# A handicap in the order of issue for two kinds of TensorE work in the attention block of a two-block network

## The chip, the cores and the metric

The kernel runs on one core of one Trainium2 chip. The metric is the device time of one execution in microseconds (us). Three runs of the kernel before gave 1686.42, 1688.52 and 1691.94 us; their median is 1688.52 us.

The engines: PE is TensorE (matmuls and transposes), DVE is VectorE, ACT is ScalarE, POOL is GpSimd, SP issues the DMAs.

## The reference

A sequence of 256 tokens of width 1024 passes two layers of a first block and then two layers of a second one, all in float32. The change lies in the first block's mixer:

```python
h = rmsnorm(x, g_pre_mix[l])
z = jnp.einsum('bsd,de->bse', h, w_in[l])
z_moba, z_fox, z_fg, z_cq, z_ckv, z_kr, z_dil = jnp.split(z, SPLIT_POINTS, axis=-1)
qa, ka = apply_rope(qa, cos_h, sin_h), apply_rope(ka, cos_h, sin_h)
o_moba = moba_attention(qa, ka, va)
log_f = jax.nn.log_sigmoid(z_fg.astype(jnp.float32) + b_forget[l].astype(jnp.float32))
cum = jnp.cumsum(log_f, axis=1).transpose(0, 2, 1)
o_fox = blocked_causal_attention(qb, kb, vb, HEAD_DIM ** -0.5, cum)
...
o_mla = blocked_causal_attention(q_full, k_full, v_c, (MLA_NOPE_DIM + MLA_ROPE_DIM) ** -0.5)
qd, kd = apply_rope(qd, cos_h, sin_h), apply_rope(kd, cos_h, sin_h)
o_dil = dilated_mixture(qd, kd, vd)
mix = jnp.concatenate([from_heads(o_moba), from_heads(o_fox), from_heads(o_mla), from_heads(o_dil)], axis=-1)
x = x + rmsnorm(jnp.einsum('bse,ed->bsd', mix, w_out[l]), g_post_mix[l])
```

There are four attentions of four heads each: moba (with 256 tokens it is plain causal attention), fox (the one with forget gates; `cum` is added to its logits), mla, and dilated. Only moba's and the dilated one's queries and keys are rotated as whole 512-column tiles.

## The kernel before, in words

The tokens are two halves `h` of 128. Each float32 factor of a large matmul is split in a high and a low part, and a product is made of three matmuls in the faster float32 form (hidden state `hX`, weights `wh` and `wl`). ACT makes the high part of a unit of weights and DVE the low part, while PE multiplies; `raw` is the DMA's landing place. Transposes, scores, value products and the running sum are in plain float32.

In `block1` (L824) the projections come in this order, each for both halves: the columns of mla with the forget gates (356), moba's queries and keys, moba's and fox's values, fox's queries and keys, mla's up-projections, the dilated queries and keys, the dilated values. A chain of its own takes each result on. `qkchain` (L917) rotates a 512-column tile on DVE into a tile `z`, takes a PSUM bank, transposes `z` in four parts on PE and copies the bank to `T` on ACT. `cumchain` (L1011) makes the log of the forget gates (`lf`, 128x8), sums it along the tokens with three small matmuls against a triangle of ones in `cs`, and copies the sum to `cum` on ACT. `foxchain` (L1046) waits for `cum` (L1058), copies it beside the keys of its half, and transposes these.

`group` (L838) is the attention of some heads of one half: scores on PE, mask added and row maximum on DVE, exponentials on ACT, reciprocal and scaling on DVE, transposes on PE, copy on ACT; `attend` (L879) follows with value products on PE and the split of the result into `mH` and `mL`. moba and dilated have two groups per half, fox and mla one in the first half and two in the second. After the projections `w_out` (L1132) multiplies with the output weights: first moba's part of half 0, then fox's part of half 0, then both of half 1, then mla's and the dilated parts.

The order on the engines is not written out. `Order` (L116) runs all chains and picks one instruction after another by the smallest key, the estimated start plus a bias; each engine then executes its instructions in that order:

```python
def push(self, task, op):
    ready = self.deps(op)
    b = op.bias() if callable(op.bias) else op.bias
    self.n += 1
    heapq.heappush(self.heap, (self.start(op, ready) + b + task.bias, ready, self.n, op, task))
```

`start` (L153) is the later of the time at which the operands are ready and the time at which the engine is free. Projection matmuls have the bias `B_MAIN` = 0.02 (us); transposes and the running sum's matmuls have 0. L292 is the matmul, L296 the transpose, L309 any ACT operation; all of a kind share one line, so tiles tell them apart.

Of the kernel before, what the change touches and what calls it, by code (L numbers as in the profile page):

```python
# [18 lines left out]
P = 128  # L19
# [13 lines left out]
CST_CAU, CST_DIL, CST_U, CST_IC = 0, 128, 384, 640  # L33
# [243 lines left out]
def body(ctx, tc, x, positions, wu, wm, wq_up, wkv_up, rows, feat, gfeat, cst, cid, out, nsub=99):  # L277
    nc = tc.nc
# [7 lines left out]
    def view(t):  # L286
        return t if isinstance(t, bass.AP) else t[:]

    def mm(o, l, r, start, stop, bias=B_MAIN, fp32=False, half=None):
        o, l, r = view(o), view(l), view(r)  # L290
        c = (4 if fp32 else 1) * r.free_size() / 2400 + 0.0027
        return Op("e", c, (o,), (l, r), lambda: nc.tensor.matmul(o, l, r, start=start, stop=stop), bias, half)  # L292

    def tr(o, i):
        o, i = view(o), view(i)
        return Op("e", 0.1094, (o,), (i,), lambda: nc.tensor.transpose(o, i, idt[:, :P]))  # L296

    def act(o, i, f, bias_=0.0, **kw):
        o, i = view(o), view(i)
        c = (0.052 if i.tensor.name.startswith("bank") else 0.093) + i.free_size() / 1200  # L300
        ins, outs = [i], [o]
        for k in ("scale", "bias"):
            if k in kw and not isinstance(kw[k], float):
                c += 0.093
                ins.append(view(kw[k]))
        if "accum_out" in kw:
            c += 0.093
            outs.append(view(kw["accum_out"]))
        return Op("a", c, outs, ins, lambda: nc.scalar.activation(o, i, f, **kw), bias_, None, f)  # L309
# [23 lines left out]
    def stt(o, a, s, b, op0, op1):  # L333
        o, a, b = view(o), view(a), view(b)
        ap = not isinstance(s, float)
        return Op("d", 0.069 + o.free_size() / 960 + 0.061 * ap, (o,), (a, b) + ((view(s),) if ap else ()),
                  lambda: nc.vector.scalar_tensor_tensor(o, a, s, b, op0=op0, op1=op1))  # L337
# [44 lines left out]
    cs = one.tile([P, CST_N], F32, name="cs")  # L382
    idt = one.tile([P, 176], F32, name="idt")
# [151 lines left out]
    def hidden(n, h, i, src, g):  # L535

        hH, hL = halves(h)
        kb = []
        for j in range(2):
            kb.append((yield banks))  # L540
        for j in range(4):
            yield tr(kb[j % 2][:, j * P:(j + 1) * P], src[:, j * P:(j + 1) * P])

        def low(kt, o):
            yield stt(hL[:, kt, :], o, g[:, kt:kt + 1], hH[:, kt, :], OP.mult, OP.subtract)
            ck.set(ck.flag("h", n, h, kt))
            if kt % 4 >= 2:
                banks.put(kb[kt % 2])

        for j in range(4):  # L550
            kt, o = 4 * i + j, kb[j % 2][:, j * P:(j + 1) * P]
            yield act(hH[:, kt, :], o, AF.Copy, scale=g[:, kt:kt + 1])
            ck.spawn(low(kt, o), bias=B_EDGE)
# [109 lines left out]
    def ffn(n_, half, nxt, fp):  # L663
# [16 lines left out]
        def tchain(h, b):  # L680
            yield ck.flag("r2", n_, h)
            s = yield scr
            yield act(s[:, :256], b[:, :256], AF.Silu, scale=r2[n_][h])
            yield mul(s[:, 256:], b[:, 256:], s[:, :256])
            banks.put(b)
            k = yield banks
            for i in range(2):
                yield tr(k[:, i * P:(i + 1) * P], s[:, 256 + i * P:256 + (i + 1) * P])
            scr.put(s)
            if 0 not in fT:  # L690
                fT[0] = yield ft_
            w = slice(h * P, (h + 1) * P)
            yield from evac_split(k[:, :256].rearrange("p (a t) -> p a t", a=2), fT[0][0][:, :, w], fT[0][1][:, :, w])
            banks.put(k)
# [111 lines left out]
    def rope(dst, src, tab, n, d, after=None):  # L806

        w = 2 * n * d
        t0 = yield scr
        u0 = yield scr  # L810
        t = t0[:, :w].rearrange("p (n a d) -> p n a d", n=n, a=2)
        u = u0[:, :w].rearrange("p (n a d) -> p n a d", n=n, a=2)
        cb = tab[:, 0].rearrange("p (o a) d -> p o a d", o=1).to_broadcast([P, n, 2, d])
        yield mul(t, src, cb)
        for a in range(2):
            sb = tab[:, 1, a:a + 1, :].to_broadcast([P, n, d])
            yield mul(u[:, :, a, :], src[:, :, 1 - a, :], sb)
        if after:
            after()
        yield add(dst, t, u)  # L820
        scr.put(t0)
        scr.put(u0)

    def block1(n_, l, ap, tabs, trope, nxt):  # L824
# [13 lines left out]
        def group(grp, h, q, k, scale, mask, PT, deps, tiled):  # L838
# [31 lines left out]
            for c in range(hb * nb):  # L870
                yield tr(tb[:, c * P:(c + 1) * P], lg[:, c * P:(c + 1) * P])
# [45 lines left out]
        def qkchain(h, b, T):  # L917
            yield tk["tab", h]
            z = yield zs
            yield from rope(z.rearrange("p (n a d) -> p n a d", n=8, a=2),  # L920
                            b.rearrange("p (n a d) -> p n a d", n=8, a=2), t64r[h], 8, 32, lambda: banks.put(b))
            tb = yield banks
            for k in range(4):
                yield tr(tb[:, k * P:(k + 1) * P], z[:, k * P:(k + 1) * P])
            zs.put(z)
            yield act(T[:, :, h * P:(h + 1) * P], tb.rearrange("p (a t) -> p a t", a=4), AF.Copy)
            banks.put(tb)
# [24 lines left out]
        lf = ap.tile([P, 8], F32, name="lf")  # L952
# [52 lines left out]
        for h in range(2):  # L1005
            b = yield from proj(n_, h, Wq, 512, 2)
            tk["mq", h] = ck.spawn(qkchain(h, b, Tm))
# [3 lines left out]
        def cumchain():  # L1011
            for h in range(2):
                yield ck.flag("fg", n_, h)
            yield stt(lf, fg, -1.0, fg, OP.mult, OP.min)
            yield act(lf, lf, AF.Exp)
            yield act(lf, lf, AF.Ln, bias=1.0)
            yield stt(lf, fg, 0.0, lf, OP.min, OP.subtract)
            ct = yield banks
            yield mm(ct[:, 0:4], cs[:, CST_U:CST_U + P], lf[:, 0:4], True, True, 0.0, True)
            yield mm(ct[:, 4:8], cs[:, CST_U + P:CST_U + S], lf[:, 0:4], True, False, 0.0, True)  # L1020
            yield mm(ct[:, 4:8], cs[:, CST_U:CST_U + P], lf[:, 4:8], False, True, 0.0, True)
            yield act(cum, ct[:, :8].rearrange("p (h n) -> p h n", h=2), AF.Copy, scale=-8.0)
            banks.put(ct)
        tcum = ck.spawn(cumchain())

        W = Units()
# [89 lines left out]
        for h in range(2):  # L1116
            b = yield from proj(n_, h, W, 512, 2)
            tk["dq", h] = ck.spawn(qkchain(h, b, Td))
# [490 lines left out]
```

## Time and profile before

| what | value |
|---|---|
| median of three runs | 1688.52 us |
| the profiled execution's own time | 1686.9 us |
| its span | 1685.1 us |
| PE busy | 1673.4 us, 99% |
| DVE busy | 1263.0 us, 75% |
| ACT busy | 1028.7 us, 61% |
| share of PE in the chain that ended last | 96% |

The span is the time from the first to the last recorded instruction of the profiled execution; 1.8 us of the time lie around it. A row of a timeline merges equal instructions that follow each other: start, length, engine, line, operation, tiles, shape and number, and in brackets the idle time before it and what ended it. A plain float32 matmul has two records, so "x8" of scores or value products are four matmuls. The matmuls overlap in the records; what one costs is read from start to start. Layer 0 of the first block runs from about 8 to 121 us, layer 1 from about 299 to 409 us.

### The profile page before, as it was taken

The page shows a single profiled execution, that of the slowest core. Times are in us where ns is not written, and L with a number is a line of the kernel's source. Part 1 is how long each engine was busy: PE and PEld are TensorE (multiplying, and loading weights), DVE is VectorE, ACT ScalarE, POOL GpSimd, SP SyncE. Part 2 cuts the span into 40 slices and gives each one's busy share as a digit, 9 for nine tenths or more (in the row PEclk, how much of TensorE's full clock was granted, in tenths as well). Part 3 has the DMA queues.
Part 4 walks back from the last instruction along what each step waited for, and adds up shares of the span by engine and source line. Part 5 has one row for each costly group of instructions (what it writes and reads, how often), then busy time and mean ns, then how long its engine had stood idle before and what let it go on. Part 6 is the DMA issues. An engine that isn't in the chain of part 4 may idle for free.

```text
span 1685.1 us, 25126 instructions
## 1 busy us (share of the span) xinstructions
PE 1673.4 (99%) x9401; PEld 1493.6 (89%) x9401; DVE 1263.0 (75%) x1943; ACT 1028.7 (61%) x1749; POOL 35.9 (2%) x73
## 2 busy tenths in 40 slices
PE   8999999999999999999999999999999999999998
PEld 7788998878999899988998899989998899889997
DVE  7878765877877597657898787668765789878763
ACT  7867654786755475546656575547554666557552
POOL 1000000100000000000000000000000000000000
PEclk9999999999999999999999999999999999999999
DMA  8347764424866476646655487637664665648650
GB/s 285 103 165 248 251 201 147 166 90 138 290 228 197 135 246 229 203 160 206 201 181 203 157 298 230 200 125 255 222 209 151 213 201 182 204 151 302 231 167 25
DMA packets 92283, 328.46 MB, mean 195 GB/s; under 512 B 11008, under 2 KB 12032, under 8 KB 91904
## 3 DMA queue, kind: packets, MB, share of 16 engines
q1 hardware_dynamic: 92160, 326.86, 58.3%
q8 instruction: 73, 1.20, 0.3%
q14 instruction: 50, 0.41, 0.1%
HBM read 325.77 MB, written 1.05 MB: 194 GB/s over the span
## 4 chain that ended last, share of the span: by engine, by line
PE 96%; ACT 1%; DMA 1%; issue 1%; DVE 1%; SPq 0%; DVEq 0%; POOLq 0%; POOL 0%; ACTq 0%
PE bank L292 93%; PE bank L296 3%; DMA raw<-in_wu_dram 1%; ACT wh L309 1%; DMA raw<-in_wm_dram 0%; DVE wl L314 0%; ACT hX L309 0%; ACT junk L309 0%; ACT L309 0%; SPq L367 0%; DVE sm L342 0%; ACT qk L309 0%; DVE x L337 0%; DVE w L314 0%; DVEq L1605 0%
## 5 line engine op out<-in xcount | busy, mean ns | idle before, releaser
L314 DVE TENSOR_TENSOR wl<-raw,wh 128x1024 fp32r<-128x1024 f32 (+1 forms) x471 | 564.6, 1207 | 141.3 <-ACT wh L309 137.1
L292 PE MATMUL bank<-hX,wh 128*128 128x512 f32 x1728 | 569.7, 382 | 0.0
L309 ACT ACTIVATE wh<-raw 128x1024 fp32r<-128x1024 f32 (+1 forms) x471 | 487.2, 1043 | 114.4 <-DMA raw<-in_wu_dram 60.8
L292 PE MATMUL bank<-hX,wl 128*128 128x256 f32 x1728 | 472.0, 273 | 0.0
L292 PEld LDWEIGHTS bank<-hX,wh 128*128 128x128 f32 x1728 | 327.2, 189 | 44.7
L292 PEld LDWEIGHTS bank<-hX,wl 128*128 128x128 f32 x1728 | 332.4, 192 | 0.8
L292 PE MATMUL bank<-wh,hX 128*128 128x512 f32 (+2 forms) x960 | 285.7, 374 | 0.8 <-ACT wh L309 0.8
L309 ACT ACTIVATE scr<-bank 128x256 f32<-128x256 f32 x288 | 108.8, 378 | 236.5 <-PE bank L292 236.3
L292 PE MATMUL bank<-hX,xh 128*128 128x512 f32 x704 | 233.0, 382 | 0.0
L292 PEld LDWEIGHTS bank<-wh,hX 128*128 128x128 f32 x960 | 177.5, 190 | 22.5 <-issue 1.5
L314 DVE TENSOR_TENSOR xl<-raw,xh 128x1024 fp32r<-128x1024 f32 x140 | 169.5, 1221 | 34.0 <-ACT xh L309 33.3
L292 PE MATMUL bank<-hX,xl 128*128 128x256 f32 x704 | 192.1, 273 | 0.0
L314 DVE TENSOR_TENSOR scr<-scr,bank 128x256 f32<-128x256 f32 x288 | 120.3, 418 | 89.7 <-ACT scr L309 89.7
L292 PE MATMUL bank<-wl,hX 128*128 128x512 f32 (+2 forms) x480 | 179.2, 373 | 0.5 <-DVE wl L314 0.5
L309 ACT ACTIVATE xh<-raw 128x1024 fp32r<-128x1024 f32 x140 | 145.7, 1052 | 14.8 <-DMA raw<-in_wu_dram 11.5
L292 PEld LDWEIGHTS bank<-hX,xh 128*128 128x128 f32 x704 | 133.3, 189 | 18.3
L292 PEld LDWEIGHTS bank<-hX,xl 128*128 128x128 f32 x704 | 135.4, 192 | 0.6
L292 PE MATMUL bank<-wh,fH 128*128 128x512 f32 x320 | 121.5, 380 | 0.0
L292 PE MATMUL bank<-wh,fL 128*128 128x512 f32 x320 | 121.5, 380 | 0.0
L292 PE MATMUL bank<-wl,fH 128*128 128x512 f32 x320 | 121.4, 380 | 0.0
L292 PEld LDWEIGHTS bank<-wl,hX 128*128 128x128 f32 x480 | 91.1, 190 | 11.3 <-DVE wl L314 1.0
L292 PE MATMUL bank<-xh,fH 128*128 128x512 f32 x208 | 79.4, 382 | 0.0
(158 smaller groups left out, 1929.7 us busy)
## 6 DMA issues: line engine op xcount, KB each, us to landing
raw<-in_wu_dram SPq DMA_DIRECT2D x596, 512.0 KB, 4.7
gpost<-in_rows_dram SPq DMA_DIRECT2D x10, 512.0 KB, 7.1
raw<-in_wm_dram SPq DMA_DIRECT2D x7, 356.0 KB, 3.8
bg<-in_rows_dram SPq DMA_DIRECT2D x2, 1024.0 KB, 4.5
x<-in_x_dram SPq DMA_DIRECT2D x4, 256.0 KB, 5.0
out_dram<-x SPq DMA_DIRECT2D x4, 256.0 KB, 2.0
raw<-in_wkv_up_dram SPq DMA_DIRECT2D x2, 256.0 KB, 3.6
raw<-in_wq_up_dram SPq DMA_DIRECT2D x2, 192.0 KB, 4.2
```

What stands on the lines that cost most here:

```text
L292: return Op("e", c, (o,), (l, r), lambda: nc.tensor.matmul(o, l, r, start=start, stop=stop), bias, half)
L296: return Op("e", 0.1094, (o,), (i,), lambda: nc.tensor.transpose(o, i, idt[:, :P]))
L309: return Op("a", c, outs, ins, lambda: nc.scalar.activation(o, i, f, **kw), bias_, None, f)
L314: lambda: nc.vector.tensor_tensor(o, a, b, op=op), bias)
```

## The change

Two handicaps are given. The first of the four transposes in `qkchain` gets the bias 0.8, and the first of the three matmuls of the running sum gets 2.0. Both are added to the estimated start when the next instruction is picked. No instruction is added or removed; the order of POOL and that of SP, so of all DMAs, is the same as before. On PE, DVE and ACT the order differs within the two layers of the first block alone.

```diff
--- before.py
+++ after.py
@@ -291,9 +291,9 @@
         c = (4 if fp32 else 1) * r.free_size() / 2400 + 0.0027
         return Op("e", c, (o,), (l, r), lambda: nc.tensor.matmul(o, l, r, start=start, stop=stop), bias, half)
 
-    def tr(o, i):
+    def tr(o, i, bias=0.0):
         o, i = view(o), view(i)
-        return Op("e", 0.1094, (o,), (i,), lambda: nc.tensor.transpose(o, i, idt[:, :P]))
+        return Op("e", 0.1094, (o,), (i,), lambda: nc.tensor.transpose(o, i, idt[:, :P]), bias)
 
     def act(o, i, f, bias_=0.0, **kw):
         o, i = view(o), view(i)
@@ -921,7 +921,7 @@
                             b.rearrange("p (n a d) -> p n a d", n=8, a=2), t64r[h], 8, 32, lambda: banks.put(b))
             tb = yield banks
             for k in range(4):
-                yield tr(tb[:, k * P:(k + 1) * P], z[:, k * P:(k + 1) * P])
+                yield tr(tb[:, k * P:(k + 1) * P], z[:, k * P:(k + 1) * P], 0.8 if k == 0 else 0.0)
             zs.put(z)
             yield act(T[:, :, h * P:(h + 1) * P], tb.rearrange("p (a t) -> p a t", a=4), AF.Copy)
             banks.put(tb)
@@ -1016,7 +1016,7 @@
             yield act(lf, lf, AF.Ln, bias=1.0)
             yield stt(lf, fg, 0.0, lf, OP.min, OP.subtract)
             ct = yield banks
-            yield mm(ct[:, 0:4], cs[:, CST_U:CST_U + P], lf[:, 0:4], True, True, 0.0, True)
+            yield mm(ct[:, 0:4], cs[:, CST_U:CST_U + P], lf[:, 0:4], True, True, 2.0, True)
             yield mm(ct[:, 4:8], cs[:, CST_U + P:CST_U + S], lf[:, 0:4], True, False, 0.0, True)
             yield mm(ct[:, 4:8], cs[:, CST_U:CST_U + P], lf[:, 4:8], False, True, 0.0, True)
             yield act(cum, ct[:, :8].rearrange("p (h n) -> p h n", h=2), AF.Copy, scale=-8.0)
```

PE, layer 0, the running sum (`lf,cs`) before: it stands within the projection of the values (`hX`).

```order
L292 MATMUL bank_135<-wh_69,hX 128x512 x2
L292 MATMUL bank_135<-wl_70,hX 128x512
L292 MATMUL bank_136<-lf,cs 128x4 x3
L292 MATMUL bank_135<-wh_69,hX 128x512
L292 MATMUL bank_135<-wh_71,hX 128x512
```

The same place of the program in the changed kernel: behind the last projection, the rotated tiles' transposes and the sixteen score products of moba and dilated (`qk_252`, `qk_257`).

```order
L292 MATMUL bank_135<-qk_257 128x256
L292 MATMUL bank_129<-qk_257 128x256
L292 MATMUL bank_136<-lf,cs 128x4 x3
L296 MATMUL bank_130<-idt,w_250 65x128 x4
L296 MATMUL bank_133<-idt,w_247 65x128 x4
L296 MATMUL bank_132<-idt,w_246 128x128 x2
```

The three matmuls moved from the 167th to the 454th place among PE's matmuls; the two sets of four transposes of fox's keys (65x128) that need the sum moved behind them.

PE, layer 0, moba's rotated tile of half 0 (`w_245`) before: its transposes stand within the projection of fox's queries and keys, and the first scores (`qk_252`) follow some rows on.

```order
L292 MATMUL bank_131<-wl_80,hX 128x512
L296 MATMUL bank_135<-idt,w_245 128x128 x4
L296 MATMUL bank_130<-idt,w_248 128x128
L292 MATMUL bank_131<-wh_79,hX 128x512
...
L292 MATMUL bank_133<-qk_252 128x128
L292 MATMUL bank_129<-qk_252 128x128
```

In the changed kernel all four rotated tiles of the layer (two of moba, two of dilated) are transposed after the last projection.

```order
L292 MATMUL bank_135<-wh_77,hX 128x256
L296 MATMUL bank_130<-idt,w_245 128x128 x4
L296 MATMUL bank_134<-idt,w_246 128x128 x4
L296 MATMUL bank_133<-idt,w_251 128x128 x4
L296 MATMUL bank_131<-idt,w_248 128x128 x4
L292 MATMUL bank_129<-qk_252 128x128
L292 MATMUL bank_135<-qk_252 128x128
```

What depended on them moved too: from the first of these transposes to the last value product PE now has 60 transposes, 27 scores and sums, 44 value products and 13 matmuls of the output projection; 71 matmuls of that projection stand behind.

PE, layer 1, the running sum in the changed kernel: behind the first seven matmuls of the output projection that follow the last dilated value product.

```order
L292 MATMUL bank_133<-wh_67,mL_2786 128x512
L292 MATMUL bank_130<-lf,cs 128x4 x3
L296 MATMUL bank_136<-idt,w_2798 65x128 x4
L296 MATMUL bank_129<-idt,w_2793 65x128 x4
L292 MATMUL bank_132<-qk_2802,qk_2801 128x128 x4
L292 MATMUL bank_134<-qk_2802,qk_2801 128x256
```

Here it moved from the 1757th to the 2091st place, and all of fox's attention stands behind it.

## Rows read from the trace of the kernel before

**Rows 1.** The page: busy by engine; TensorE's clock, tenths; weight splits on ACT.
```profile
PE 1673.4 (99%) x9401; PEld 1493.6 (89%) x9401; DVE 1263.0 (75%) x1943; ACT 1028.7 (61%) x1749; POOL 35.9 (2%) x73
...
PEclk9999999999999999999999999999999999999999
...
L309 ACT ACTIVATE wh<-raw 128x1024 fp32r<-128x1024 f32 (+1 forms) x471 | 487.2, 1043 | 114.4 <-DMA raw<-in_wu_dram 60.8
```

**Rows 2.** Timeline of PE, both layers: start us, length us, what, [idle before].
```profile
33.46 0.83 PE L292 MATMUL bank<-lf,cs 128*128 128x4 f32 x6 [0.37 <-DVE lf L337]
...
338.69 0.78 PE L296 MATMUL bank<-idt,w 128*128 128x128 f32 x3 [0.90 <-DVE w L331]
```

**Rows 3.** Timelines of ACT and DVE, layer 0: running sum, first reader.
```profile
34.33 0.18 ACT L309 ACTIVATE cum<-bank 128x8 f32<-128x8 f32 x1 [0.75 <-PE bank L292]
...
48.84 0.16 DVE L350 COPY w<-cum 128x4 f32<-128x4 f32 x1
```

**Rows 4.** Timeline of PE: value products between projections, and a long run.
```profile
79.89 0.59 PE L292 MATMUL bank<-wh,hX 128*128 128x512 f32 x2
80.41 0.66 PE L292 MATMUL bank<-w,vc 128*64 128x128 f32 x8
81.00 0.48 PE L292 MATMUL bank<-wl,hX 128*128 128x512 f32 x1
81.32 0.60 PE L292 MATMUL bank<-wh,hX 128*128 128x512 f32 x2
...
342.86 1.52 PE L292 MATMUL bank<-w,vmf 128*64 128x128 f32 x22
344.31 0.48 PE L292 MATMUL bank<-wh,hX 128*128 128x512 f32 x1
```

**Rows 5.** Timeline of DVE, layer 0: the softmax of the four dilated groups.
```profile
97.49 1.95 DVE L314 TENSOR_TENSOR w<-bank,cs 128x256 f32<-128x256 f32 x4
99.35 1.92 DVE L342 TENSOR_REDUCE sm<-w 128x2 f32<-128x256 f32 x4
101.19 0.37 DVE L331 TENSOR_SCALAR sm<-sm 128x2 f32<-128x2 f32 x4
101.47 1.22 DVE L314 TENSOR_TENSOR wl<-raw,wh 128x1024 fp32r<-128x1024 f32 x1
102.60 0.16 DVE L346 RECIPROCAL sm<-sm 128x2 f32<-128x2 f32 x1
102.80 0.48 DVE L331 TENSOR_SCALAR w<-w,sm 128x128 f32<-128x128 f32 x2
...
105.30 0.62 DVE L331 TENSOR_SCALAR w<-w,sm 128x256 f32<-128x256 f32 x2
```

**Rows 6.** Timeline of ACT, layer 0: the same four groups.
```profile
101.45 0.40 ACT L309 ACTIVATE w<-w,sm 128x128 f32<-128x128 f32 x1 [3.43 <-DVE sm L331]
...
103.00 0.49 ACT L309 ACTIVATE w<-w,sm 128x256 f32<-128x256 f32 x1
...
106.09 0.60 ACT L309 ACTIVATE w<-bank 128x512 f32<-128x512 f32 x1 [0.50 <-PE bank L296]
```

**Rows 7.** Timeline of PE, layer 0: dilated scores, transposes, row after its values.
```profile
96.49 1.58 PE L292 MATMUL bank<-qk 64*128 64x128 f32 x16
98.00 0.48 PE L292 MATMUL bank<-wh,mH 128*128 128x512 f32 x1
...
103.93 0.38 PE L296 MATMUL bank<-idt,w 128*128 128x128 f32 x2
...
110.81 0.48 PE L292 MATMUL bank<-wh,mL 128*128 128x512 f32 x1
```

**Rows 8.** Timeline of PE, layer 1: four forget-gate score products, eleven transposes.
```profile
352.42 1.89 PE L292 MATMUL bank<-qk,qk 65*128 65x256 f32 x8
354.15 1.37 PE L296 MATMUL bank<-idt,w 128*96 128x128 f32 x11
355.27 0.41 PE L292 MATMUL bank<-wh,mH 128*128 128x384 f32 x1
```

## The prediction

> **What bounds the kernel now.** I read the page first: PE is busy 99% of the span, DVE 75%, ACT 61%, and TensorE's granted clock is at its upper level in every slice [rows 1]. So the time is the sum of PE's rows, and a change of order can win only what PE now loses between them, and can lose whatever it makes PE wait. Then the timeline of PE through both layers of block 1, for idle time and for rows that cost more than their kind. Idle at the two kinds of work that the change touches is small: 0.37 us before the running sum of layer 0 (in layer 1 PE reaches it without waiting), and 0.90 us in layer 1 before the transposes of a softmax that follows from a rotated tile [rows 2]. The transposes of the rotated tiles themselves wait nowhere. Then the sum's reader: it is made at 34.33 and first read at 48.84 [rows 3], so it has 14.5 us to spare, and delaying it by two would cost nothing.
>
> **What the handicap really does.** The key is the estimated start plus the bias, and the start of anything that is ready is the moment PE comes free. A projection that is ready has that same start and a bias of 0.02. So 0.8 or 2.0 is no delay of that length: the row loses against every ready projection, each time it is compared, until PE would otherwise stand still for that long. The order shows it: the sum falls back 287 places in layer 0 and 334 in layer 1, and all rotated tiles are transposed after the last projection. With them moba, fox and the dilated attention, which had been spread among projections, are pressed into the end of the block. I call the stretch from there to the last value product the tail.
>
> **What it saves.** (a) Waits: 0.37 and 0.90, 1.3 us in all. (b) Switching on PE between float32 products and the split matmuls. Four value products between projections take 0.59 us, eleven in a run 1.45, so each costs 0.123 and a visit 0.10 besides; entering costs 0.52 instead of the 0.44 of two matmuls at 0.22, and the first matmul behind is 0.10 late: 0.29 a visit [rows 4]. (The 0.22: 27 matmuls of the output projection fill 98.00 to 103.93 [rows 7].) The order counts 27 borders between the two kinds in each layer before and 13 and 14 now, 13.5 visits fewer: 3.9 us. Borders between transposes and products rise by 5; no row prices one alone; between 0 and a whole visit's 0.29 I take 0.1, as most lie in runs that cost nothing visible: minus 0.5. Together 4.7 us saved, if PE never waits in the tail. Transposes cost the same alone or in runs (eleven in 1.12 us [rows 8], 0.11 with the late start of the row behind).
>
> **What it costs: PE's own rows in the tail.** Layer 0: 60 transposes at 0.11 (6.6), sixteen moba and dilated scores (twice the 1.51 of rows 7: 3.0), fox's scores (four long 1.73 [rows 8], four of half the length 0.9), the sum (0.7), 44 value products at 0.123 (5.4), 13 projection matmuls (2.9), ten visits (2.9): 24.1 us. Layer 1 has 15 projection matmuls and eleven visits: 24.8 us.
>
> **DVE and ACT in the same stretch.** One softmax after the other now stands on DVE. The dilated one's four groups cost it 1.86 (masks), 1.84 (maxima), 0.28, four times 0.2 (reciprocals) and two pairs each of 0.4 and 0.55 (the lengths less the 0.08 by which rows overlap): 6.7 us [rows 5]. moba masks half as many columns in half 1 (minus 0.6): 6.1. fox, at the same 1.2 ns a column: 2.3 for half 0 and 3.5 for half 1. ACT has 24 exponentials at 0.39 or 0.49 (10.6 us), thirteen copies of 512 columns at 0.5 [rows 6], and some twenty shorter ones: about 23. So three engines have 20 to 24 us of work each in one stretch, in chains that pass from one to the next; none can cover for the others, and only 13 to 15 filler matmuls are left.
>
> - *Layer 0.* ACT comes out of a weight split (1.04 [rows 1]) and copies four transposed tiles; the first scores reach DVE 3.2 us into the tail. DVE then has 18.6 of softmax, three result splits at 0.31 (a mask of that shape) and two small copies: 19.8. I add 2.4 for waits, since a result split stands ahead of four groups' rows and reciprocals stand ahead of masks while ACT works through the exponentials: the last scaling ends at 25.4. From there to the end of the values took 105.9 to 110.8 before, 4.9 us [rows 5, 7]. The tail is 30 us, PE's rows 24.1: 6 us idle.
> - *Layer 1.* First scores at 2.6; moba and dilated 12.8, two result splits 0.6, a weight split 1.13 [rows 5], waits 1.2: last scaling at 18.3, values done at 23.2, seven projection matmuls to 24.7. Only then the running sum, and everything of fox is behind it, alone: sum 0.7, ACT's copy 0.35, copy 0.2, transposes 0.45, copy 0.55, scores 0.9, mask 0.6, maximum 0.6, 0.1, four exponentials 1.55, reciprocal 0.2, scaling 0.8, transposes 0.45, copy 0.55, values 0.55, and about 0.15 for each of eight handovers: 9.7; half 1, whose exponentials follow on ACT, ends 3.3 later: 13 us. The tail is 37.7, PE's rows 24.8: 13 us idle.
>
> What was hidden and is no longer: the 14.5 us of slack of the sum [rows 3], since the projections that covered it are used up. The matmuls of w_out behind the tail need weights that are split by then, so nothing is late after it. SP's and POOL's orders are unchanged.
>
> **The sum.** 6 + 13 - 4.7 = 14.3 us on the profiled execution's 1686.9, which is 1.6 below the median of the runs (that is under their spread of 5.5, so nothing is added): 1701.2, said as **1701**.
>
> **Bounds of the idle time.** Below: DVE and ACT without any wait. Then PE's own rows bound both tails but for the first 3 and last 3 us, and fox's chain alone has 13 - 8.8: 10 us in all, 5.3 over before (1692). Above: the dilated four groups took 96.49 to 110.81, 14.3 us [rows 7]; eleven groups at that rate are 39 us, eight and fox's chain 42: 32 us idle, 1714. I stand nearer the lower end, because those 14.3 us held 38 projection matmuls that the tail does not.
>
> **The clock.** PE's longest idle in these layers is now 0.90 us, and the granted clock never left 2.4 GHz [rows 1, 2]. My tail has single waits of 1 to 2 us, six or more in a row in layer 1; no row shows whether that is borne. The Trainium skill (TensorE: Matmul & The Clock Gate, "HAM oscillation — how this bites in real kernels") warns that idle gaps between bursts of matmuls send the clock to half rate. By that rule the sum would be that of the third rival; by the row it stays.
>
> **Rivals.**
> 1. *The tail keeps PE fed* (faster). If DVE and ACT kept pace, the idle time would be under 4.7 us and the switches win: 1682 with none. The point that decides is 2.3 us idle a layer. For it: DVE and ACT are 25% and 39% idle overall. Against: fox's chain in layer 1 has nothing beside it.
> 2. *Half the idle time.* PE idles about 9 us: 1691, not to be told from no change. For it: in-order engines overlap groups better than my waits.
> 3. *The clock falls* in layer 1's tail. The 8.8 us of PE's rows in fox's part and the 15 us of w_out behind them would run at 1.2 GHz for a part: 5 to 15 us on top, 1711 as its middle.
> 4. *The handicap changes nothing that matters*, a row slipping by 0.8 or 2 us: excluded by the order.
>
> **Chances.** A measurement here can tell about 0.3%, 5 us. Forecast (1694 to 1707) 0.66; rival 1 0.06; rival 2 0.15; rival 3 0.13. Of the forecast and rival 3 nearly all is slower by over 5 us: slower 0.78, same 0.16, faster 0.06. The range leaves out rival 1 and the far end of rival 3: 1690 to 1714.
>
> **What would show it.** Right: PE idle of about 6 us in layer 0 between some 78 and 108 us, about 13 in layer 1 between 367 and 405, released by DVE's scaling (L331) and ACT's copies (L309) of `w` and `qk`; fewer idle spots before the tail; 71 and 69 matmuls of w_out at 0.22 behind; the rest of the span unchanged but shifted. Wrong: PE busy without gaps through the tails (rival 1 or 2), a granted clock under 1 there (rival 3), or new waits outside block 1.

## The result and the profile after

The changed kernel takes 1708.15 us (median of four runs, 1707.6 to 1708.6), the kernel before on the same chip 1688.12 us. The ratio is 1.0119 with a 95% interval of 1.0106 to 1.0131: 20.0 us slower. The profiled execution took 1708.6 us, its span is 1706.8 us, 21.7 more than before.

The page of the changed kernel, against [rows 1]: PE's busy time rose by 11.7 us although it executes the same 9401 rows, and one of the forty slices shows a granted clock under 9 tenths.

```profile
PE 1685.1 (99%) x9401; PEld 1499.1 (88%) x9401; DVE 1261.4 (74%) x1943; ACT 1027.3 (60%) x1749; POOL 37.0 (2%) x73
...
PEclk9999999998999999999999999999999999999999
```

Where the time went follows from comparing when PE starts the same places of the program (starts in the two traces, after less before; where the tails begin, the two orders have issued different rows, so those places are not compared):

| place | delay, us |
|---|---|
| block 1, layer 0, behind the first projections | 0.4 |
| end of the output projection, layer 0 (126.95) | 6.1 |
| layer 1 begins | 6.1 |
| end of the output projection, layer 1 (430.69) | 21.7 |
| last matmul of the kernel | 21.7 |

So all but 0.4 us arises in block 1: 5.7 us in layer 0 and 15.6 us in layer 1. The rest of the kernel is only shifted. The 0.4 us lie in the start-up, whose order did not change: in this execution PE waited there once for the DMA of `x`, 1.99 us, instead of 1.43 and 0.50 us, and the granted clock was 0.50 from 8.67 to 12.08 us, which it was not in the profile before.

What PE waited for in the changed kernel, the whole span (engine, line, releaser: us in total, times, longest us). DVE's scaling (L331) and ACT's copies (L309) lead, both new at this size:

```profile
PE bank L296 <- DVE w L331: 5.1, 5, 2.3
PE bank L292 <- ACT qk L309: 3.0, 5, 1.2
...
PE bank L296 <- DVE w L350: 1.9, 2, 1.4
...
PE bank L296 <- DVE w L354: 1.1, 1, 1.1
PE bank L292 <- ACT w L309: 0.7, 1, 0.7
```

L350 is the copy of the running sum into fox's key tile. PE waited nowhere for it before, since its reader came 14.5 us after the sum [rows 3]; now PE waits 1.40 and 0.47 us for it.

The timeline of PE through both tails of the changed kernel (start us, length us, what, [idle before]). The first row is the start of layer 0's tail, and the row at 111.50 is the first behind its last value product; 373.87 and 415.67 are the same places of layer 1:

```profile
78.59 1.91 PE L296 MATMUL bank<-idt,w 128*128 128x128 f32 x16
...
86.69 0.83 PE L292 MATMUL bank<-lf,cs 128*128 128x4 f32 x6
88.92 2.10 PE L296 MATMUL bank<-idt,w 128*65 128x128 f32 x14 [1.40 <-DVE w L350]
92.20 3.82 PE L292 MATMUL bank<-qk,qk 65*128 65x128 f32 x16 [1.19 <-ACT qk L309]
...
97.00 3.25 PE L296 MATMUL bank<-idt,w 128*128 128x128 f32 x14
99.90 0.78 PE L292 MATMUL bank<-wh,mH 128*128 128x512 f32 x1
...
111.50 0.48 PE L292 MATMUL bank<-wl,mH 128*128 128x512 f32 x1
...
373.87 1.47 PE L296 MATMUL bank<-idt,w 128*128 128x128 f32 x12
...
382.35 1.14 PE L292 MATMUL bank<-qk 64*128 64x256 f32 x8 [1.02 <-ACT qk L309]
383.99 0.99 PE L296 MATMUL bank<-idt,w 128*128 128x128 f32 x4 [0.50 <-DVE w L331]
386.34 0.70 PE L296 MATMUL bank<-idt,w 128*128 128x128 f32 x4 [1.36 <-DVE w L331]
...
399.86 0.73 PE L292 MATMUL bank<-lf,cs 128*128 128x4 f32 x6
401.06 1.09 PE L296 MATMUL bank<-idt,w 128*65 128x128 f32 x8 [0.47 <-DVE w L350]
402.39 2.89 PE L292 MATMUL bank<-qk,qk 65*128 65x128 f32 x16 [0.24 <-ACT qk L309]
407.53 1.06 PE L296 MATMUL bank<-idt,w 128*128 128x128 f32 x4 [2.25 <-DVE w L331]
...
415.67 0.48 PE L292 MATMUL bank<-wh,mH 128*128 128x512 f32 x1
```

The tails last 32.9 and 41.8 us. Besides the waits in brackets there is a second thing: at 97.00 fourteen transposes take 2.90 us to the next row's start, 0.21 each, where eleven took 1.12 before, 0.10 each [rows 8]. The sixteen records of fox's scores last 3.82 us in layer 0 (92.20), 2.89 in layer 1 (402.39).

Busy time by stretch in the changed kernel, both tails cut where the clock changes (stretch, its length, PE, PEld, DVE, ACT, POOL, then the granted clock, DMA share, GB/s):

```profile
78.60:94.00 15.40, 12.43 (x98) 9.62 (x97) 13.46 (x43) 11.61 (x39) 0.00 (x0) 1.00 0.51 173
94.00:100.83 6.83, 6.83 (x30) 5.49 (x29) 5.15 (x21) 4.64 (x15) 0.00 (x0) 0.50 0.00 0
100.83:111.50 10.67, 10.67 (x92) 7.19 (x90) 5.15 (x19) 7.80 (x27) 0.00 (x0) 1.00 0.01 2
373.90:387.55 13.65, 9.99 (x74) 6.58 (x72) 11.65 (x37) 10.80 (x35) 0.00 (x0) 1.00 0.53 188
387.55:394.38 6.83, 6.36 (x30) 4.28 (x31) 5.32 (x19) 4.68 (x16) 0.00 (x0) 0.50 0.17 53
394.38:408.03 13.65, 10.68 (x83) 8.45 (x79) 5.36 (x17) 6.39 (x22) 0.00 (x0) 1.00 0.04 14
408.03:414.86 6.83, 6.05 (x30) 3.95 (x29) 2.80 (x11) 3.32 (x10) 0.00 (x0) 0.50 0.00 0
```

In three stretches of the tails, one in layer 0 and two in layer 1, the granted clock is 0.50, 1.2 instead of 2.4 GHz. Each follows waits of PE: 1.40 and 1.19 us in layer 0; 1.02, 0.50 and 1.36 us, then 2.25 us, in layer 1. PE counts as busy there because its rows are longer. So the page's higher busy time is no more work; it hides part of the loss.

Two explanations fit what is seen so far: PE waits for the softmax that the starved rows pushed together, or PE itself runs dearer rows, at half clock. The runs below take them apart, and also ask which handicap made the loss, and whether the size of a handicap matters at all.

### The profile page after: what moved, and what is told of

Same layout as the page of the kernel before. It is cut to its first block, busy times and chain, and to the rows that moved or that the text cites. A ratio compares the mean times of both kernels' runs of the same rounds, so it can differ in the third digit from the quotient of the medians.

```text
span 1706.8 us, 25154 instructions
## 1 busy us (share of the span) xinstructions
PE 1685.1 (99%) x9401; PEld 1499.1 (88%) x9401; DVE 1261.4 (74%) x1943; ACT 1027.3 (60%) x1749; POOL 37.0 (2%) x73
## 3 DMA queue, kind: packets, MB, share of 16 engines
HBM read 325.77 MB, written 1.05 MB: 191 GB/s over the span
## 4 chain that ended last, share of the span: by engine, by line
PE 94%; DVE 2%; ACT 1%; DMA 1%; issue 1%; SPq 0%; DVEq 0%; POOLq 0%; POOL 0%; ACTq 0%
PE bank L292 92%; PE bank L296 2%; DVE wl L314 1%; ACT w L309 1%; DMA raw<-in_wu_dram 1%; ACT wh L309 0%; DVE w L314 0%; DVE sm L342 0%; DMA raw<-in_wm_dram 0%; DVE w L331 0%; DVE scr L314 0%; SPq L367 0%; ACT qk L309 0%; ACT hX L309 0%; ACT junk L309 0%
## 5 line engine op out<-in xcount | busy, mean ns | idle before, releaser
L292 PE MATMUL bank<-hX,wh 128*128 128x512 f32 x1728 | 569.8, 382 | 0.0
L309 ACT ACTIVATE wh<-raw 128x1024 fp32r<-128x1024 f32 (+1 forms) x471 | 486.3, 1042 | 129.8 <-DMA raw<-in_wu_dram 70.1
L292 PE MATMUL bank<-hX,wl 128*128 128x256 f32 x1728 | 471.5, 273 | 0.0
L292 PEld LDWEIGHTS bank<-hX,wh 128*128 128x128 f32 x1728 | 326.6, 189 | 45.2
L292 PEld LDWEIGHTS bank<-hX,wl 128*128 128x128 f32 x1728 | 331.7, 192 | 0.9
L292 PE MATMUL bank<-wh,hX 128*128 128x512 f32 (+2 forms) x960 | 283.5, 372 | 0.0
L309 ACT ACTIVATE scr<-bank 128x256 f32<-128x256 f32 x288 | 109.0, 378 | 230.3 <-PE bank L292 230.2
L292 PE MATMUL bank<-hX,xh 128*128 128x512 f32 x704 | 233.0, 382 | 0.0
L292 PEld LDWEIGHTS bank<-wh,hX 128*128 128x128 f32 x960 | 177.6, 190 | 21.3 <-issue 0.3
L292 PE MATMUL bank<-hX,xl 128*128 128x256 f32 x704 | 191.9, 273 | 0.0
L292 PE MATMUL bank<-wl,hX 128*128 128x512 f32 (+2 forms) x480 | 178.6, 372 | 0.5 <-DVE wl L314 0.5
L309 ACT ACTIVATE xh<-raw 128x1024 fp32r<-128x1024 f32 x140 | 145.7, 1052 | 13.5 <-DMA raw<-in_wu_dram 11.3
L292 PEld LDWEIGHTS bank<-hX,xh 128*128 128x128 f32 x704 | 133.1, 189 | 18.6
L292 PEld LDWEIGHTS bank<-hX,xl 128*128 128x128 f32 x704 | 135.1, 192 | 0.6
L292 PE MATMUL bank<-wh,fH 128*128 128x512 f32 x320 | 121.4, 379 | 0.0
L292 PE MATMUL bank<-wl,fH 128*128 128x512 f32 x320 | 121.3, 379 | 0.0
L292 PE MATMUL bank<-wh,fL 128*128 128x512 f32 x320 | 121.3, 379 | 0.0
L292 PEld LDWEIGHTS bank<-wl,hX 128*128 128x128 f32 x480 | 91.2, 190 | 11.4 <-DVE wl L314 1.0
L292 PE MATMUL bank<-xh,fH 128*128 128x512 f32 x208 | 79.3, 381 | 0.0
```

## The experiments

Ratios are to the kernel before, whose runs were taken beside them on the same chip (its median was 1687.3 to 1687.6 us each time), with 95% intervals.

### One handicap at a time

The sum alone:

```diff
-                yield tr(tb[:, k * P:(k + 1) * P], z[:, k * P:(k + 1) * P], 0.8 if k == 0 else 0.0)
+                yield tr(tb[:, k * P:(k + 1) * P], z[:, k * P:(k + 1) * P], 0.0)
```

> Only the running sum of the forget gates has its 2.0; the rotated tiles' transposes are back at 0. In the order the sum stands behind the last projection in both layers (490th and 2067th matmul), with the fox attention behind it, while the first (causal) attention and the transposes of the dilated one stand among the projections as before. Theory (PE waits in the tail that the starved rows make, in proportion to the softmax work pushed there): one attention more than before is in each tail, so about half of the changed kernel's loss of 20 us: 8 to 12 us over the kernel before, 1696 to 1700 us, about 3 to 7 us of waits of PE in each layer, released by DVE and ACT in fox's chain. Rival A (it is the sum alone: fox's chain of 13 us at the end): 15 us or more over before, 1703 to 1708 us. Rival B (it is the rotated tiles alone): within 3 us of before.

1696.21 us, ratio 1.0055 (1.0039 to 1.0072): 8.6 us over the kernel before, as the theory had it. Rival B falls; rival A, which wanted 15, falls too. Its timeline of PE shows fox's chain in the open, released by the same copies of DVE (L350) and ACT:

```profile
94.19 3.51 PE L296 MATMUL bank<-idt,w 128*65 128x128 f32 x16 [1.55 <-DVE w L350]
...
386.39 1.52 PE L296 MATMUL bank<-idt,w 128*65 128x128 f32 x12 [1.50 <-DVE w L350]
389.01 2.02 PE L292 MATMUL bank<-qk,qk 65*128 65x128 f32 x12 [1.10 <-ACT qk L309]
```

The granted clock is 0.50 here too, for 3.4 us behind these waits in each layer, so the 8.6 us hold a part of the clock's.

The rotated tiles alone:

```diff
-            yield mm(ct[:, 0:4], cs[:, CST_U:CST_U + P], lf[:, 0:4], True, True, 2.0, True)
+            yield mm(ct[:, 0:4], cs[:, CST_U:CST_U + P], lf[:, 0:4], True, True, 0.0, True)
```

> Only the rotated tiles' transposes have their 0.8; the running sum is back at 0, at its old place (167th and 1753rd matmul), and fox's scores and softmax stand among the projections; the causal and the dilated attention both stand behind the last projection. Theory: again about half of the 20 us: 6 to 12 us over the kernel before, 1694 to 1700 us; this and the run with the sum alone add up to 15 to 25 us. Rival A (the sum alone): within 3 us of before, since fox's chain is back in its old place. Rival B (rotated tiles alone): 15 us or more over before.

1701.51 us, ratio 1.0085 (1.0070 to 1.0100): 13.9 us over before. That is 2 us above what the theory allowed, though its interval (11.8 to 16.9 us) reaches down to the theory's 12. Rival A falls; rival B is not excluded by this run's interval, but the run before excludes it. The two losses add up to 22.5 us, the change's 20.0 within the intervals. Here the largest item is one long wait in each layer, all transposes of a softmax behind DVE's scaling. In layer 0 this execution also waited 1.35 us for the running sum's operands, where it was 0.37 before:

```profile
35.57 0.83 PE L292 MATMUL bank<-lf,cs 128*128 128x4 f32 x6 [1.35 <-DVE lf L337]
...
100.86 3.43 PE L296 MATMUL bank<-idt,w 128*128 128x128 f32 x12 [3.10 <-DVE w L331]
...
393.67 3.42 PE L296 MATMUL bank<-idt,w 128*128 128x128 f32 x12 [3.03 <-DVE w L331]
```

Behind each of the long waits twelve transposes take over 3 us: the granted clock is 0.50 for 3.4 us again, from 100.91 and from 394.46 on.

### The size of the handicap

```diff
-                yield tr(tb[:, k * P:(k + 1) * P], z[:, k * P:(k + 1) * P], 0.8 if k == 0 else 0.0)
+                yield tr(tb[:, k * P:(k + 1) * P], z[:, k * P:(k + 1) * P], 0.03 if k == 0 else 0.0)
...
-            yield mm(ct[:, 0:4], cs[:, CST_U:CST_U + P], lf[:, 0:4], True, True, 2.0, True)
+            yield mm(ct[:, 0:4], cs[:, CST_U:CST_U + P], lf[:, 0:4], True, True, 0.03, True)
```

> Both handicaps set to 0.03, a little above the 0.02 that every projection matmul carries, instead of 0.8 and 2.0. In the order both kinds of rows again stand behind the last projection (the sum 414th and 1999th). Theory (what counts is only that a ready projection is always preferred; the size of the handicap is no delay): a loss like the changed kernel's, 10 to 20 us over before, 1697 to 1708 us; the lower end is possible because the sum now goes first in the tail and fox's chain runs beside the other two softmaxes instead of alone behind them. Rival (a handicap costs by its size: 0.03 us is a fortieth of what the change gave): within 2 us of before, 1686 to 1690 us.

1701.85 us, ratio 1.0086 (1.0071 to 1.0101): 14.3 us over before. A handicap of 0.03 makes most of the loss that 0.8 and 2.0 made. In the profiled executions layer 0 lost 7.5 us and layer 1 8.0 us, where the change lost 5.7 and 15.6. What differs in layer 1 is the place of the sum: here it is at the start of the tail, at 376.59 in the next rows, and fox's scores run at 385.62 beside the other two attentions instead of alone from 399.86 on. The granted clock is 0.50 for 6.8 us in layer 0 and for 10.2 us in layer 1. Its timeline of PE:

```profile
99.66 1.09 PE L296 MATMUL bank<-idt,w 128*128 128x128 f32 x4 [3.19 <-DVE w L331]
...
376.59 0.73 PE L292 MATMUL bank<-lf,cs 128*128 128x4 f32 x6
...
385.62 2.89 PE L292 MATMUL bank<-qk,qk 65*128 65x128 f32 x16 [0.42 <-ACT qk L309]
...
393.31 2.96 PE L296 MATMUL bank<-idt,w 128*128 128x128 f32 x10 [1.73 <-DVE w L331]
```

The same two lines with 0.01 in place of 0.03:

> Both handicaps set to 0.01, a little below the 0.02 of the projections' matmuls. In the order everything is back where it was before but for a few rows (the sum 167th and 1757th). Theory (starvation has a threshold, and it is the 0.02 of the projections): within 2 us of the kernel before, 1685.5 to 1689.5 us, though 0.03 cost 14. Rival (the loss grows smoothly with the handicap's size): a third of the 14 us of the run with 0.03, about 1692 us.

1687.74 us, ratio 1.0002 (0.9993 to 1.0011): no change. Between 0.01 and 0.03 the loss goes from nothing to 14 us. So the handicap has a threshold between the two, where the key puts it at the projections' 0.02, and it is not the length of a delay.

### PE kept at work in the waits

The changed kernel, its order untouched; when the order reaches one of eleven places, transposes of a constant are issued into the PSUM bank that the next row overwrites:

```diff
+FILL = {430: 2, 457: 12, 471: 10, 2027: 9, 2031: 4, 2035: 12, 2039: 5, 2045: 3, 2094: 6, 2102: 2, 2110: 20}
...
+            if op.e == "e":
+                self.pe += 1
+                for _ in range(FILL.get(self.pe, 0)):
+                    self.filler(op.outs[0])
             op.fn()
...
+    ck.filler = lambda o: nc.tensor.transpose(o[:, :P], idt[:, :o.shape[0]], idt[:, :P])
```

> The changed kernel in its own order, with 85 more transposes of a constant on PE (0.11 us each at full clock), put ahead of eleven rows of the two tails that wait for DVE or ACT, 2 to 20 to a place and no more than fit into the wait; each is written over by the row behind it. Theory (waits of PE of about 16 us and, on top of them, three stretches of 6.8 us at half clock that follow such waits, which cost about 10 us): the half-clock stretches in the tails go or shrink, and the time falls by 5 to 10 us to 1698 to 1703 us, although PE has more to do. Rival (waits on DVE and ACT alone make the loss, and the half clock is hidden in them): the time stays within 3 us of 1708, and it rises by up to 9 us if the extra rows stand in the way.

1703.76 us, ratio 1.0098 (1.0083 to 1.0113): 3.5 us less than the changed kernel by the ratios, though PE does 85 transposes more. The two intervals together leave about 3 us of uncertainty either way. The theory's 5 to 10 us were not reached in the whole time, which by itself can hardly tell theory and rival apart; the traces can. The clock does not fall in the tails any more. Busy time by stretch, the two tails:

```profile
80.70:110.80 30.10, 29.68 (x242) 22.22 (x240) 23.57 (x80) 23.43 (x79) 0.00 (x0) 1.00 0.27 89
373.30:412.30 39.00, 35.47 (x280) 26.91 (x278) 25.19 (x80) 25.12 (x80) 0.00 (x0) 1.00 0.25 80
```

The tails are 30.1 and 39.0 us long instead of 32.9 and 41.8, 5.6 us together. The whole span gained 3.3 us, less than that, because this execution lost 2.1 us before the first tail, 0.7 in the start-up and 1.4 in a wait of PE for a copy of ACT's (`vc`) at 58 us. The timeline of PE shows the filled places, and in its last two rows waits in layer 1 that the changed kernel did not have there (the added transposes have line L396; L300, L304, L317 and L339 are L292, L296, L309 and L331 of the changed kernel):

```profile
89.46 1.50 PE L396 MATMUL bank<-idt 128*65 128x128 f32 x12
91.00 2.10 PE L304 MATMUL bank<-idt,w 128*65 128x128 f32 x14
92.93 1.26 PE L396 MATMUL bank<-idt 128*128 128x128 f32 x10
94.29 2.89 PE L300 MATMUL bank<-qk,qk 65*128 65x128 f32 x16
...
97.69 1.81 PE L304 MATMUL bank<-idt,w 128*128 128x128 f32 x14
...
391.42 0.48 PE L300 MATMUL bank<-wh,mH 128*128 128x512 f32 x1 [0.54 <-ACT mH L317]
...
409.70 0.44 PE L304 MATMUL bank<-idt,w 128*128 128x128 f32 x2 [1.17 <-DVE w L339]
```

The rows that took 3.82 (the end of it at half clock) and 3.25 us take 2.89 and 1.81 here. So both explanations hold a part: 5.6 us is the clock, by one execution of each kernel, and the larger part is waiting. In the 20.5 us at half clock PE was busy for 19.2 us; at full clock these rows could take 9.6 us less at most. So a good half of that came back. Some of the rest is waiting now: the last two rows waited 0.54 and 1.17 us for ACT and DVE, where at half clock PE came later and did not wait.

### Less work for DVE in the softmax

Both kernels, each in its own order, without the scaling rows:

```diff
-                yield ts(l3[:, i, :], l3[:, i, :], rc[:, i:i + 1], None, OP.mult)
+                o_ = ts(l3[:, i, :], l3[:, i, :], rc[:, i:i + 1], None, OP.mult); o_.fn = lambda: None; yield o_
```

> The changed kernel in its own order, without the multiplications by the inverse row sums on DVE (the softmax of block 1's three attentions is left unnormalised; 24 such rows in each tail, 6.4 us of DVE in each). Theory (DVE and ACT's softmax sets the length of the tails): the waits of PE for these rows (5.1 us in five waits in the second layer) shrink, and the kernel is 4 to 12 us faster than the changed one, 1696 to 1704 us. Rival (the loss is made by PE itself, its rows at half clock and their dearer order): within 2 us of 1708.

> The kernel before in its own order, without the same multiplications (the softmax of block 1's three attentions is left unnormalised). Theory (before, the softmax lies beside the projections and is covered): within 1.5 us of the kernel before, 1686 to 1689 us; what the changed kernel gains by the same cut is then the part of DVE that the change uncovered. Rival (block 1's softmax was on the path before already): 4 us or more faster than before, as in the changed kernel.

The changed kernel without them: 1702.83 us, ratio 1.0092 (1.0077 to 1.0108), 5.3 us faster than the changed kernel by the medians, 4.6 by the ratios. The kernel before without them: 1687.12 us, ratio 0.9997 (0.9987 to 1.0006), nothing. The cut that the old order hides the new order shows: the softmax has come onto the path, as the theory had it, and the rival falls. How much of the 5.3 us is DVE's own can't be said, since the half-clock stretch of layer 0 is gone too, and layer 0 gained 2.6 us, about what the clock had cost there; the two of layer 1 are 3.4 us long instead of 6.8. What PE waits for shows the next in line, ACT in place of DVE's scaling:

```profile
PE bank L292 <- ACT qk L309: 3.3, 5, 1.5
PE bank L292 <- ACT w L309: 2.5, 2, 1.4
...
PE bank L296 <- DVE w L350: 1.9, 2, 1.4
...
PE bank L296 <- ACT w L309: 0.9, 2, 0.6
```

### A handicap that runs out

What a handicap of 0.8 or 2.0 us would do if it were one. The bias is counted from the moment the row is offered and is zero once that time is over:

```diff
-                yield tr(tb[:, k * P:(k + 1) * P], z[:, k * P:(k + 1) * P], 0.8 if k == 0 else 0.0)
+                yield tr(tb[:, k * P:(k + 1) * P], z[:, k * P:(k + 1) * P], (lambda l=ck.now + 0.8: max(0.0, l - ck.now)) if k == 0 else 0.0)
...
-            yield mm(ct[:, 0:4], cs[:, CST_U:CST_U + P], lf[:, 0:4], True, True, 2.0, True)
+            yield mm(ct[:, 0:4], cs[:, CST_U:CST_U + P], lf[:, 0:4], True, True, (lambda l=ck.now + 2.0: max(0.0, l - ck.now)), True)
```

> The change's own numbers, 0.8 and 2.0, but as a handicap that runs out: a row is held back until 0.8 or 2.0 us after the moment it asked, then it has 0 again. In the order the sum slips by only 9 and 15 places (to the 176th and 1772nd matmul), all attention rows stay among the projections, and changes between projections and attention rows fall from 27 to 19 in the first layer and from 27 to 26 in the second. Theory (the loss comes from the starvation alone, what the words of the change say is harmless): no tail, no half clock behind the start, and 1 to 2 us faster than before for the shorter wait of the sum (0.37 us) and the fewer changes (0.29 us for two): 1685 to 1688 us, which is at the edge of what can be measured. Rival (holding these rows back costs by itself, starved or not): 3 us or more slower than before, over 1690.5 us.

1683.61 us, ratio 0.9974 (0.9964 to 0.9983): 4.4 us faster than before by the ratio (3.7 by the medians) and 24 us faster than the changed kernel. The direction is the theory's, the size about twice its upper end of 2 us. The waits of PE over its whole span, all that are listed, have neither the sum's 0.37 nor more than a fifth of a microsecond of the 0.90 of [rows 2]:

```profile
PE bank L296 <- DMA x<-in_x_dram: 1.9, 1, 1.9
PE bank L292 <- DVE mhalf L1431: 1.2, 1, 1.2
PE bank L296 <- DVE w L331: 0.2, 1, 0.2
```

Most of the rest is price, not waiting: in layer 0 the 96 records of the value products take 7.1 us from start to start instead of 8.7, and the 240 projection matmuls of 512 and 256 columns 49.2 instead of 50.5. The products stand in longer runs.

The same edit with 16.0 in place of 0.8, and with the two halves apart:

> As the run before, with the rotated tiles' transposes held back until 16 us after they asked, the sum until 2.0 us. In the order the changes between projections and attention rows fall to 21 and 16, the attention is later by up to 16 us but only the usual last part stands behind the last projection. Theory: 2 to 4 us faster than before (17 changes fewer at 0.29 us for two make 2.5 us, the sum's wait 0.37): 1683.5 to 1685.5 us. Rival (any delay of the attention shows in the end, because its softmax is pushed towards the tail): slower than before by 2 us or more, with waits of PE behind the last projection.

1691.40 us, ratio 1.0025 (1.0015 to 1.0034): the theory fell, the rival was right. Fewer changes between kinds did not help, as rows came late for their readers again. Its timeline of PE (of the slowest of its ten runs, 1694.99 us) has the waits in layer 0's middle, behind which the granted clock is 0.50 from 59.86 to 66.68, and at the end of block 1 in both layers, where the last dilated values now come behind nearly all of the output projection:

```profile
59.53 3.49 PE L292 MATMUL bank<-qk,qk 65*128 65x256 f32 x8 [1.40 <-ACT qk L309]
...
125.09 1.58 PE L292 MATMUL bank<-w,vd 128*64 128x128 f32 x16 [0.57 <-DVE hX L337]
...
414.74 1.96 PE L292 MATMUL bank<-w,vd 128*64 128x128 f32 x16 [1.91 <-ACT w L309]
```

> Only the rotated tiles' transposes with the handicap that runs out after 0.8 us, the sum at 0 in its old place. The run with both was 4.4 us faster than before, where 1 to 2 were expected; this asks which part made it. Theory (the value products and projections lie together in longer stretches: the changes between projections and attention rows are 19 and 26 as in the run with both): 3 to 4.5 us faster than before, 1683 to 1684.5 us. Rival (it was the sum, whose wait is gone and which lets the rows behind it pass): within 1 us of before.

1683.81 us, ratio 0.9976 (0.9967 to 0.9985): 4.1 us faster by the ratio. Most of the gain is that of the rotated tiles, and the rival falls.

> Only the sum with the handicap that runs out after 2.0 us, the transposes at 0. In the order the sum slips by 9 and 10 places, nothing else moves but for the rows it passes. Theory: its wait of 0.37 us in the first layer is gone and nothing else, 0 to 0.6 us faster than before, 1686.5 to 1687.5 us. Rival (the sum made the gain of the run with both): 3 us or more faster.

1686.10 us, ratio 0.9991 (0.9982 to 1.0000): 1.5 us faster by the ratio, more than the 0 to 0.6 expected, though its interval (0 to 3.0) does not tell the two apart; the rival's 3 is at its very end.

> The transposes held back until 1.5 us instead of 0.8 us after they asked, the sum until 2.0 us. Changes between projections and attention rows: 21 and 23 (with 0.8 us: 19 and 26). Theory (the gain goes by these changes, one fewer in the two layers together): within 1.5 us of the run with 0.8 and 2.0, 1682 to 1685 us. Rival (every us of delay pushes the attention towards the tail, as the run with 16 us, which lost 4 us): 1686 us or more.

1683.93 us, ratio 0.9976 (0.9968 to 0.9985): as with 0.8, and the rival falls. That the gain goes by the changes between projections and attention rows is not shown by this: 44 of them against 45 can't be told apart, and with 16 us there were 37 and the kernel lost.

## Why the prediction was right, and where it was not

- **A bias is no delay.** Right, and shown from three sides: 0.03 starves and loses 14 us, 0.01 does nothing, and the same 0.8 and 2.0 with an end gain 4 us.
- **PE's idle time in the tails, 6 and 13 us.** The lengths came out right: at full clock the tails last 30.1 and 39.0 us (forecast 30 and 37.7). Less PE's own rows, costed at 24.1 and 24.8, that leaves 6.0 and 14.2. How much of it is idle time is not shown. Only 3.0 and 7.9 us stand as idle in the changed kernel's stretches; the rest lies in gaps between rows that the records' lengths cover, or in rows dearer than I costed them, and was not separated.
- **The releasers.** DVE's scaling and ACT's copies, as forecast. The copy behind the sum (L350) is a third that I had in fox's chain, but did not name as a wait.
- **What was hidden and is no longer.** Shown for the sum: its handicap alone costs 8.6 us, though it had 14.5 us of slack [rows 3]. That fox's chain stands alone at the end of layer 1 is the visible difference from the run with 0.03, which lost 8.0 instead of 15.6 us there; no run tried it by itself.
- **What it saves, 4.7 us.** 4.5 is left over when the tails' 20.2, the clock's 5.6 and the start-up's 0.4 are taken from 21.7. It is a remainder, taken with the costed rows, and proves no single item. The wait of 0.90 in layer 1 gave place to one of 1.05 (mla's transposes for L354). And a visit is no constant: with 0.8 and 2.0 us that run out, 4.5 visits fewer (9 borders) and 1.1 us less waiting gave 4.4 us, about 0.7 a visit instead of 0.29; with 16 us there were 8.5 visits fewer, and new waits made it a loss.
- **The clock.** This is the step that failed: "no row shows whether that is borne ... by the row it stays", so it entered the sum with nothing, on the strength of one wait of 0.90 us that had left the clock alone, and the third rival had it in layer 1 alone, at 0.13. It fell in both layers and cost 5.6 us, 2.8 in each tail (their lengths against those with the waits filled), near the lower end of the rival's 5 to 15. The output projection behind the tails, which the rival had slow for a part, ran at full clock, 0.218 us a matmul. The rule of the Trainium skill (TensorE: Matmul & The Clock Gate, "HAM oscillation — how this bites in real kernels"), that idle gaps between bursts halve the clock, agrees with the trace: 0.50 granted behind waits of 1.40 and 1.19 us, of 1.02, 0.50 and 1.36 us, and of 2.25 us.
- **The sum.** 14.3 was forecast on the profiled execution, and 21.7 came there (20.0 between the medians). Of the 7.4 us between them the clock is 5.6, the longer tails 1.2, the start-up 0.4 and the smaller saving 0.2; as the saving is a remainder, these add up by construction. 1708 lies within the range, above the forecast's own 1694 to 1707 and below the 1711 of the third rival: forecast and rival happened together, and should not have been weighed as alternatives.
- **The other rivals.** That the tail keeps PE fed (1682) or half fed (1691) is excluded by the time.
- **What would show it.** 71 and 69 matmuls of the output projection behind the tails took 0.218 each (15.45 and 15.02 us), as said; new waits outside block 1 did not appear. The sign named for the third rival, a granted clock under 1, came too, in both layers. The tail of layer 1 stood from 374 to 416, not from 367 to 405: the layer before it ended later, and it is longer itself.

## What to carry to other kernels

In a list scheduler that picks the smallest estimated start, a constant bias decides who wins a tie, not how late a row may be; above the bias of a stream that is always ready, any value starves the row until that stream is used up. Give a preference an end (here 0.8 and 2.0 us counted from the offer, 4 us faster than before instead of 20 slower), and look in the order at how many places a row falls, not at the number that was written. When a change opens waits on TensorE, put the clock into the sum and not only among the rivals. To see what half clock really costs, fill the waits and compare the stretches: here 5.6 of at most 9.6 us came back, as some of that time would have been waited anyway.

## What was not expected of the hardware

- The granted clock fell to 1.2 GHz after waits as short as 1.40 and 1.19 us (layer 0), with transposes and scores between them. With the same waits filled by transposes it stayed at 2.4 GHz in both tails. The length of a wait does not decide it alone: in the run with the rotated tiles alone 1.35 us (up to 35.57) left it at 2.4 GHz, in the run with 16 us 1.40 us (up to 59.53) was followed by 1.2 GHz from 59.86 on.
- Three half-clock stretches, 20.5 us in all, cost 5.6 us, not the 9.6 that half the busy time in them would make.
- The start-up, whose order is the same everywhere, ran at 1.2 GHz for 3.4 us in eleven of the fourteen profiles and for 6.8 us in one; in the kernel before and in the changed kernel without the scaling rows it did not.
- The price of changing between value products and projections is not one number: in layer 0 of the bounded order 96 records of value products took 7.1 us, before 8.7. Why, beyond their standing in longer runs, was not tried.
